# Norm sums one chunk later in layer 0, and an end with a fixed order and its norm weights on GpSimd

## The chip, the cores and the metric

One NeuronCore of a Trainium2 chip runs the whole program in one launch. The metric is the device time of one execution in microseconds. Engine names here are PE (TensorE, matmuls), DVE (VectorE), ACT (ScalarE), POOL (GpSimd) and SP (SyncE, which only issues DMAs). Each engine works through its own queue in the order in which the program was built, and waits at an instruction until the semaphores named there have been raised.

## The reference

512 tokens of width 1024 go through two layers and a last norm. All is float32.

```python
# layer 0: h += conformer_conv(rmsnorm(h)); h += swiglu_ffn(rmsnorm(h))
# shared K/V from rmsnorm(h); layer 1: h += attention; h += swiglu_ffn(rmsnorm(h))
def rmsnorm(x, g):
    return x * lax.rsqrt(jnp.mean(x * x, axis=-1, keepdims=True) + EPS) * g
def swiglu_ffn(x, w_up, w_down):
    gate, up = jnp.split(x @ w_up, 2, axis=-1)
    return (jax.nn.silu(gate) * up) @ w_down      # inner width 2816
return rmsnorm(h, norm_final)
```

## The kernel before

The residual stream lies transposed in `hT` (channels on the partitions, tokens along the free axis) until the last layer's FFN, where blocks of it are flipped to tokens on the partitions. Weights come in chunks of 128 x 1024 floats (0.5 MB) in the order of one list, `PLAN`. SP loads a chunk nine places ahead into one of six `raw` buffers. Three places ahead each chunk is split in two float32r parts: ACT casts the high part (`whi`, L294), DVE subtracts to get the low part (`wlo`, L297), into four buffers each. A product is then three matmuls (`mm3`, L380 to L382: high x high, high x low, low x high). Chunks of the first part (`NATIVE`, which ends with the first pair of FFN up-chunks) are not split and use one plain float32 product (L378).

RMSNorm is not applied to the FFN's input. The matmuls work on the unscaled stream, and the scale goes into the evictions. `Rms` makes it in steps: `add` squares each of the eight channel tiles on ACT (L487) and adds it to a running sum (L491, on DVE for this norm). `step1` sums over the partitions with matmuls against a column of ones (L503), makes mean plus epsilon on DVE (L505), takes the power -1/2 on POOL (L507) and, for 256 tokens, puts the scales on two diagonal matrices on ACT (L515). `spread` multiplies these with a matrix of ones (L529), so that each partition has every token's scale, and `step2` copies that to SBUF (L523).

Layer 0's first FFN runs on 256 tokens at a time. For the first half of the tokens (`ffn_part(0, 0, ...)`, not `twin`) `ffn_up` goes over pairs of column blocks; a pair has four chunks (two halves of the inner dimension times gate and up), 24 matmuls each when split. The first pair's eviction is held in `pending`, and done inside the second pair: `step1` stands behind the first pair, and the evictions, with the spread, behind the second chunk of the second pair (line 697). At the same time DVE, ACT and POOL make the depthwise convolution of the other half of the tokens (L1010 on DVE, L1002 on ACT, L1003 on POOL, squares and sums L1039 to L1045), and POOL issues DMAs that add weight blocks in memory (L289), which a counter spreads over the chunks.

The second half of the tokens (`twin`) and layer 1 use other paths; the diff leaves them as they are.

At the very end layer 1's last pair is multiplied out with tokens on the partitions. For each of four blocks of 128 tokens and each of two halves of 512 channels (`g`) PE makes six matmuls into a bank (L1600). DVE scales it and adds the residual (L1602). ACT squares it and sums along the row (L1604). DVE makes the mean from both halves (L1606, L1608), POOL the power (L1610). DVE multiplies by the norm's weights (L1611), and the scale goes on last, one half on ACT (L1617), the other on DVE (L1615), each followed by its output DMA (L1618) from ACT's queue or SP's. No order is written down there: a scheduler put the instructions of the four blocks into each engine's queue by its own estimates.

Of the kernel before, what the change touches and what calls it, by code (L numbers as in the profile page):

```python
# [11 lines left out]
F32 = mybir.dt.float32  # L12
F32R = mybir.dt.float32r
AF = mybir.ActivationFunctionType
ALU = mybir.AluOpType
# [3 lines left out]
P = 128  # L19
D = 1024  # L20
# [8 lines left out]
NBLK = S // P  # L29
BAND = 2 * P  # L30
NBUCKET = 32
EPS = 1e-6
# [177 lines left out]
def hybrid_trunk(ctx: ExitStack, tc: tile.TileContext, xT, W, prm_in, wdw_in, sinks, relb, onehot, fin, lead, out):  # L210
    nc = tc.nc
    cpool = ctx.enter_context(tc.tile_pool(name="const", bufs=1))
    quads = ctx.enter_context(tc.tile_pool(name="quads", bufs=11))
    wpool = ctx.enter_context(tc.tile_pool(name="wts", bufs=4))
    tmp = ctx.enter_context(tc.tile_pool(name="tmp", bufs=5))
    small = ctx.enter_context(tc.tile_pool(name="small", bufs=4))
# [15 lines left out]
    def temp():  # L232
        return tmp.tile([P, 512], F32, tag="tmp", name=uid("tmp"))
# [128 lines left out]
    def get(*key):  # L362
        advance()
        pace()
        due[0] += rate[0]
        tick(int(due[0]))
        due[0] -= int(due[0])
        i = stream["use"]
        assert PLAN[i] == key, (PLAN[i], key)
        stream["use"] += 1  # L370
        hi, lo = splits.pop(i)
        n = {"kv": 4, "up": 4, "q": 4}.get(key[0], 2)
        sh = dict(a=n)
        return tuple(w and w.rearrange("p (a b) -> p a b", **sh) for w in (hi, lo))
# [95 lines left out]
    mhalf = cpool.tile([P, 4], F32, tag="mhalf", name="mhalf")  # L470
# [414 lines left out]
    def rows_of(g, t):  # L885
        return hT[:, g * 4:(g + 1) * 4, t * P:(t + 1) * P]
# [386 lines left out]
    class Rows0:  # L1273

        rms = None
# [46 lines left out]
    nxt = Next(("kv", "mix1"))  # L1322
# [5 lines left out]
    for pair, a in part2_products():  # L1328
        if pair not in open_pairs:
            c = z0.tile([P, 2, 2, 2, 256], F32, tag="z0", name=uid("up"), bufs=5)  # L1330
# [5 lines left out]
        c = open_pairs[pair].gates()  # L1336
# [15 lines left out]
    if True:  # L1352
# [6 lines left out]
        x, rms = nxt.x, nxt.rms  # L1359
# [8 lines left out]
        for half in range(2):  # L1368
            whi, wlo = get("kv", 0, half)
# [7 lines left out]
        for half in range(2):  # L1377
            whi, wlo = get("kv", 1, half)
            for k in range(4):
                xh, xl = xkv[half * 4 + k]  # L1380
# [4 lines left out]
            if half == 0:  # L1385
                rs_bc = rms.step2()
                rs = rms.rs
# [133 lines left out]
        for part in range(2):  # L1521
            for g in range(2):
# [3 lines left out]
                if part == 0:  # L1526
# [19 lines left out]
                for m in range(4):  # L1546
                    i = g * 4 + m
                    nc.vector.tensor_add(h[i], banks[m], h[i])
                    nxt.on_h(i)
            if part == 0:  # L1550
# [4 lines left out]
                nxt = Rows("ffn1", pool7)  # L1555
# [12 lines left out]
    for kind, pair in STEPS1:  # L1568
# [6 lines left out]
        if by_seven(1, pair):  # L1575
            c = seven_pair("up", pair, nxt, new_gates(pool7), flip if pair == SEVENS[0] else None)
# [11 lines left out]
        nc.sync.dma_start(gain, fin.to_broadcast([P, D]))  # L1588

    whole = [get("down", 1, LAST, g) for g in range(2)]  # L1590
    for b in range(NBLK):
        tok, rs = slice(b * P, (b + 1) * P), nxt.rms.rs[:, b:b + 1]
        room = quads.tile([P, 4, 512], F32, tag="quad", name=uid("room"))
        ss = small.tile([P, 4], F32, tag="ss", name=uid("ss"))
        for g, (whi, wlo) in enumerate(whole):
            acc = bank()
            for k in range(2):
                xh, xl = (hid[:, e, k, tok] for e in range(2))
                for n, (x, w) in enumerate(((xh, whi), (xh, wlo), (xl, whi))):
                    nc.tensor.matmul(acc, x, w[:, k, :], start=k == 0 and n == 0, stop=k == 1 and n == 2)  # L1600
            v, o = room[:, g], room[:, 2 + g]
            nc.vector.scalar_tensor_tensor(v.rearrange("p (i c) -> p i c", i=4), acc.rearrange("p (i c) -> p i c", i=4), rs,  # L1602
                                           rows_of(g, b), op0=ALU.mult, op1=ALU.add)
            nc.scalar.activation(temp(), v, AF.Square, accum_out=ss[:, g:g + 1])  # L1604
            if g == 0:
                nc.vector.tensor_scalar(ss[:, 2:3], ss[:, 0:1], 1.0 / D, EPS, op0=ALU.mult, op1=ALU.add)  # L1606
            else:
                nc.vector.scalar_tensor_tensor(ss[:, 3:4], ss[:, 1:2], 1.0 / D, ss[:, 2:3], op0=ALU.mult, op1=ALU.add)  # L1608
                last = small.tile([P, 1], F32, tag="rs1", name=uid("rs1"))
                nc.gpsimd.tensor_tensor(last, ss[:, 3:4], mhalf[:, 0:1], op=ALU.pow)  # L1610
            nc.vector.tensor_mul(o, v, gain[:, g * 512:(g + 1) * 512])  # L1611
        for g in range(2):
            o = room[:, 2 + g]
            if g:
                nc.vector.tensor_scalar(o, o, last[:, 0:1], None, op0=ALU.mult)  # L1615
            else:
                nc.scalar.mul(o, o, last[:, 0:1])  # L1617
            (nc.sync if g else nc.scalar).dma_start(out[tok, g * 512:(g + 1) * 512], o)  # L1618
    seven.close()


# [25 lines left out]
```

## Time and profile before

| | |
|---|---|
| median of 3 runs | 1046.09 us (1045.9 to 1046.29) |
| profiled execution | 1048.36 us |
| its span, first to last instruction | 1046.6 us |
| granted TensorE clock, mean | 0.997 |
| PE / DVE / ACT / POOL busy | 1032.7 / 779.1 / 612.7 / 466.6 us |
| instructions | 17683 |

In a timeline row the first number is the start in us from the span's start, the second the length from the first to the last of the merged instructions; then engine, line, operation, what is written and read, shape, and the count. Square brackets give the idle time of the engine ahead of the row and what ended it. In the rows for one tile three numbers stand for the shortest, the median and the longest duration in ns. In the list of waits the columns are the total in us, the number of times and the longest one.

### The profile page before, as it was taken

To read this page: it belongs to the slowest core of one execution; us is meant where nothing else is said; L and a number is where in the kernel's file an instruction comes from. 1 tells how busy PE (TensorE), PEld (TensorE's weight loads), DVE (VectorE), ACT (ScalarE), POOL (GpSimd) and SP (SyncE) were. 2 spreads that over 40 slices of the span, in tenths; PEclk is the share of its full clock that TensorE was granted. 3 is DMA by queue.
4 is the path that set the end of the run, shared out by engine and by line. 5 is a ranking of instruction groups with operands and counts; after the bars stand their busy time and mean duration, and the time that the engine had idled before them with its cause. 6 is when DMAs were issued, how large, how long until landed. Compare 5 with 4: busy or idle time off the path is not lost.

```text
span 1046.6 us, 17683 instructions
## 1 busy us (share of the span) xinstructions
PE 1032.7 (99%) x6574; PEld 932.7 (89%) x6574; DVE 779.1 (74%) x1206; ACT 612.7 (59%) x1060; POOL 466.6 (45%) x563
## 2 busy tenths in 40 slices
PE   9999998999999999999999999999999999999996
PEld 8888887999988999998888877788989999898995
DVE  3999989978889786773536556678686877868677
ACT  3887896946776565552334555466655555554653
POOL 3999998940444332222214255405442334334131
PEclk9999999999999999999999999999999999999998
DMA  9999846989899988898968776845879888867742
GB/s 351 335 332 195 203 130 173 282 245 272 243 256 253 302 221 283 255 296 251 284 222 240 208 192 183 211 167 150 251 234 312 284 264 266 244 232 222 226 142 80
DMA packets 67282, 248.33 MB, mean 237 GB/s; under 512 B 7579, under 2 KB 13884, under 8 KB 66364
## 3 DMA queue, kind: packets, MB, share of 16 engines
q1 hardware_dynamic: 53804, 199.96, 54.7%
q0 software_dynamic: 12672, 46.14, 24.6%
q8 instruction: 51, 0.84, 0.3%
q10 hardware_dynamic: 720, 1.10, 0.3%
q14 instruction: 35, 0.29, 0.1%
HBM read 241.93 MB, written 97.52 MB: 324 GB/s over the span
## 4 chain that ended last, share of the span: by engine, by line
PE 91%; DVE 4%; ACT 2%; issue 1%; DMA 1%; POOL 1%; SPq 0%; DVEq 0%; ACTq 0%
PE bank L380 20%; PE bank L382 20%; PE bank L381 20%; PE bank L903 9%; PE bank L961 8%; PE bank L412 4%; PE bank L413 2%; PE bank L1442 1%; PE bank L1484 1%; PE bank L1471 1%; DVE bank L1010 1%; ACT pr L1002 1%; PE bank L1059 1%; DVE wlo L297 1%; DMA both<-in_lead_dram 1%
## 5 line engine op out<-in xcount | busy, mean ns | idle before, releaser
L297 DVE TENSOR_TENSOR wlo<-raw,whi 128x1024 fp32r<-128x1024 f32 x246 | 327.1, 1337 | 137.7 <-ACT whi L294 126.9
L294 ACT CAST whi<-raw 128x1024 fp32r<-128x1024 f32 x246 | 257.2, 1049 | 280.9 <-PE bank L381 194.9
L380 PE MATMUL bank<-quad,whi 128*128 128x256 f32 (+1 forms) x976 | 307.2, 317 | 0.0
L381 PE MATMUL bank<-quad,whi 128*128 128x256 f32 (+1 forms) x976 | 306.6, 315 | 0.0
L382 PE MATMUL bank<-quad,wlo 128*128 128x256 f32 (+1 forms) x976 | 305.7, 315 | 0.0
L380 PEld LDWEIGHTS bank<-quad,whi 128*128 128x128 f32 x976 | 185.5, 191 | 12.8 <-issue 1.6
L381 PEld LDWEIGHTS bank<-quad,whi 128*128 128x128 f32 x976 | 186.0, 191 | 11.8 <-issue 0.5
L382 PEld LDWEIGHTS bank<-quad,wlo 128*128 128x128 f32 x976 | 185.6, 191 | 11.8 <-issue 0.4
L854 POOL TENSOR_TENSOR up<-up 128x512 f32<-128x512 f32 x34 | 62.9, 1851 | 283.6 <-ACT up L851 283.6
L1003 POOL TENSOR_TENSOR pr<-pr,pr 128x256 f32<-128x256 f32 x208 | 157.5, 837 | 4.5 <-ACT pr L1002 4.2
L380 PE MATMUL bank<-rows,whi 128*128 128x256 f32 x488 | 138.0, 283 | 0.0
L381 PE MATMUL bank<-rows,whi 128*128 128x256 f32 x488 | 137.8, 282 | 0.0
L382 PE MATMUL bank<-rows,wlo 128*128 128x256 f32 x488 | 137.8, 282 | 0.0
L1010 DVE SCALAR_TENSOR_TENSOR bank<-apad,wdw,bank 128x256 f32<-128x256 f32 x248 | 112.4, 484 | 3.4
L1002 ACT ACTIVATE pr<-apad,wdw 128x256 f32<-128x256 f32 x208 | 98.5, 502 | 15.1 <-POOL pr L1003 13.2
L961 PE MATMUL bank<-quad,w 128*128 128x256 f32 x448 | 98.7, 380 | 0.0
L961 PEld LDWEIGHTS bank<-quad,w 128*128 128x128 f32 x448 | 84.9, 190 | 11.8 <-DVE bank L1010 0.2
L380 PEld LDWEIGHTS bank<-rows,whi 128*128 128x128 f32 x488 | 93.1, 191 | 0.3
L381 PEld LDWEIGHTS bank<-rows,whi 128*128 128x128 f32 x488 | 93.1, 191 | 0.3
L382 PEld LDWEIGHTS bank<-rows,wlo 128*128 128x128 f32 x488 | 93.0, 191 | 0.0
L491 POOL TENSOR_TENSOR tmp<-tmp,tmp 128x256 f32<-128x256 f32 (+1 forms) x28 | 26.8, 956 | 101.9 <-ACT tmp L487 96.7
L412 PE MATMUL bank<-quad,whi 128*128 128x512 f32 x168 | 59.7, 398 | 0.0
(229 smaller groups left out, 1632.9 us busy)
## 6 DMA issues: line engine op xcount, KB each, us to landing
raw<-in_W_dram SPq DMA_DIRECT2D x170, 512.0 KB, 5.7
raw<-sum SPq DMA_DIRECT2D x88, 512.0 KB, 5.5
sum<-in_W_dram SPq DMA_DIRECT2D x52, 512.0 KB, 6.3
sum<-in_W_dram POOLq DMA_DIRECT2D x44, 512.0 KB, 9.5
sum<-sum POOLq DMA_DIRECT2D x44, 512.0 KB, 8.8
sum<-in_W_dram SPq DMA_DIRECT2D x4, 3584.0 KB, 29.7
w<-in_W_dram SPq DMA_DIRECT2D x14, 512.0 KB, 9.7
sum<-in_W_dram SPq DMA_DIRECT2D x4, 1024.0 KB, 29.6
```

The lines of the kernel that those rows point to most:

```text
L294: on_act = nc.scalar.copy(hi, src).ins
L297: latest[:] = [on_act, lo_engine[0].tensor_sub(lo, src, f32(hi)).ins]
L380: nc.tensor.matmul(out, w[0], x[0], start=start, stop=False, **kw)
L381: nc.tensor.matmul(out, w[0], x[1], start=False, stop=False, **kw)
L382: nc.tensor.matmul(out, w[1], x[0], start=False, stop=stop, **kw)
L412: nc.tensor.matmul(first[2], first[0], first[1], start=start, stop=False)
L854: pool_op(nc.gpsimd.tensor_mul(gate, gate, c[:, m, :, 1, :]))
L903: nc.tensor.matmul(out, x, w[:, ws], start=first and e == 0 and i == 0, stop=e == 1 and i == 2, skip_group_check=True)
L961: mm = nc.tensor.matmul(self.pb[:, w * W2:(w + 1) * W2], w1_of(ct, w, k), x[k] if x else xg[k][:, tok], start=k == 0, stop=k == KT - 1)
L1002: on_act = nc.scalar.mul(pr, a[:, j:j + W2], tap(j))
L1003: on_pool = pool_op(nc.gpsimd.tensor_add(pr, acc, pr))
L1010: on_dve = nc.vector.scalar_tensor_tensor(yt if i == nd - 1 else c, src, tap(i), c if i else self.shift, op0=ALU.mult, op1=ALU.add)
```

## The change

In `ffn_up`, when a first pair is pending, `step1` now stands behind the first chunk of the second pair instead of behind the first pair, and the pending evictions (with the spread) behind its third chunk instead of its second. The path for `twin` keeps its places.

The end is rewritten. `piece` makes the matmuls of one block's half or part of it, and each engine's instructions there are chained (`tc.issue_after`) in the order of the program text: PE, DVE, ACT and POOL each get a fixed order. The last block's second half is split into two pieces of 256 channels, with a bank, an eviction and a sum of squares each, so the mean has three steps there. The norm weights of the first three blocks, both halves, are multiplied by POOL; those of the last block stay on DVE. A block's scaling and output stand two blocks later in the text. Outputs leave from SP's queue, but for the last block's first half, which leaves from ACT's.

```diff
-                    if half == 0 and which == 1:
-                        if w == 512 or twin:
-                            rms.step1()
+                    if twin and half == 0 and which == 1 or pending and half + which == 0:
+                        rms.step1()
+                    if half == 1 and which == 0:
                         for p in pending:
                             evac(*p)
                         pending = []
-            if w == 256 and pair == lo and not twin:
-                rms.step1()
+            if pair == lo and not twin:
                 pending.append((pair, full))
...
+    def piece(b, g, i0, i1):
+        room, ss, _ = blocks[b]
+        cols, rs = slice(i0 * P, i1 * P), nxt.rms.rs[:, b:b + 1]
+        acc = bank()[:, 0:(i1 - i0) * P]
...                                   # the six matmuls, after order["t"]
+        v, s = room[:, g, cols], ss[:, g + i0 // 2:g + i0 // 2 + 1]
+        then("v", lambda: nc.vector.scalar_tensor_tensor(...))        # was L1602
+        then("s", lambda: nc.scalar.activation(temp()[:, cols], v, AF.Square, accum_out=s))   # was L1604
...                                   # mean (DVE), power (POOL) as before, by then()
+    def weigh(b, g, eng, op):
+        room = blocks[b][0]
+        then(eng, lambda: op(room[:, 2 + g], room[:, g], gain[:, g * 512:(g + 1) * 512]))
+    def scale(b, g):
+        o, last = blocks[b][0][:, 2 + g], blocks[b][2]
+        if g:
+            then("v", lambda: nc.vector.tensor_scalar(o, o, last[:, 0:1], None, op0=ALU.mult))
+        else:
+            then("s", lambda: nc.scalar.mul(o, o, last[:, 0:1]))
+        (nc.sync if g or b < ends else nc.scalar).dma_start(out[...], o)
+    for b in range(NBLK):
+        blocks.append([...])
+        if b > 1:
+            scale(b - 2, 0)
+        piece(b, 0, 0, 4)
+        if b:
+            mean(b - 1, 1)
+        if b < ends:
+            weigh(b, 0, "p", nc.gpsimd.tensor_mul)
+        if b:
+            power(b - 1, 1)
+        if b == ends:
+            break
+        piece(b, 1, 0, 4)
+        mean(b, 0)
+        weigh(b, 1, "p", nc.gpsimd.tensor_mul)
+        if b > 1:
+            scale(b - 2, 1)
+    scale(ends - 2, 1)
+    piece(ends, 1, 0, 2)
+    piece(ends, 1, 2, 4)
+    weigh(ends, 0, "v", nc.vector.tensor_mul)
+    for n in range(3):
+        mean(ends, n)
+    power(ends, 2)
+    scale(ends - 1, 0)
+    weigh(ends, 1, "v", nc.vector.tensor_mul)
+    scale(ends - 1, 1)
+    scale(ends, 0)
+    scale(ends, 1)
```

In the built order PE's L503 stands 24 matmuls later than before and L529 24 matmuls later as well; DVE's queue is the same up to L505 and beyond it to the first eviction. In ACT's queue one L294 and two L1002 stand ahead of L515 that stood behind it, and in POOL's queue two L289 stand ahead of L507 behind the pair of L1014 where one did.

More of the change, by code (lines that the diff above doesn't have):

```diff
@@ L1590, in hybrid_trunk @@
     whole = [get("down", 1, LAST, g) for g in range(2)]
-    for b in range(NBLK):
[L1592 to L1618, printed above, removed]
@@ new lines, in hybrid_trunk, with then @@
+    order = {}
+    def then(eng, op):
+        with tc.issue_after(order[eng]) if eng in order else nullcontext():
+            order[eng] = op().ins
+    blocks, ends = [], NBLK - 1
+    def piece(b, g, i0, i1):
+        room, ss, _ = blocks[b]
+        cols, rs = slice(i0 * P, i1 * P), nxt.rms.rs[:, b:b + 1]
+        whi, wlo = whole[g]
+        acc = bank()[:, 0:(i1 - i0) * P]
+        with tc.issue_after(order["t"]) if "t" in order else nullcontext():
+            for k in range(2):
+                xh, xl = (hid[:, e, k, b * P:(b + 1) * P] for e in range(2))
+                for n, (x, w) in enumerate(((xh, whi), (xh, wlo), (xl, whi))):
+                    mm = nc.tensor.matmul(acc, x, w[:, k, cols], start=k == 0 and n == 0, stop=k == 1 and n == 2)
+        order["t"] = mm.ins
+        v, s = room[:, g, cols], ss[:, g + i0 // 2:g + i0 // 2 + 1]
+        then("v", lambda: nc.vector.scalar_tensor_tensor(
+            v.rearrange("p (i c) -> p i c", c=P), acc.rearrange("p (i c) -> p i c", c=P), rs,
+            rows_of(g, b)[:, i0:i1], op0=ALU.mult, op1=ALU.add))
+        then("s", lambda: nc.scalar.activation(temp()[:, cols], v, AF.Square, accum_out=s))
@@ new lines, in mean, with power @@
+    def mean(b, n):
+        ss = blocks[b][1]
+        if n == 0:
+            then("v", lambda: nc.vector.tensor_scalar(ss[:, 4:5], ss[:, 0:1], 1.0 / D, EPS, op0=ALU.mult, op1=ALU.add))
+            return
+        then("v", lambda: nc.vector.scalar_tensor_tensor(ss[:, 4 + n:5 + n], ss[:, n:n + 1], 1.0 / D, ss[:, 3 + n:4 + n],
+                                                         op0=ALU.mult, op1=ALU.add))
+    def power(b, n):
+        blocks[b][2] = last = small.tile([P, 1], F32, tag="rs1", name=uid("rs1"))
+        then("p", lambda: nc.gpsimd.tensor_tensor(last, blocks[b][1][:, 4 + n:5 + n], mhalf[:, 0:1], op=ALU.pow))
@@ new lines, in weigh @@
+    def weigh(b, g, eng, op):
[7 more added lines that the diff above has]
+            then("s", lambda: nc.scalar.mul(o, o, last[:, 0:1]))
+        (nc.sync if g or b < ends else nc.scalar).dma_start(out[b * P:(b + 1) * P, g * 512:(g + 1) * 512], o)
```

2 lines of the change are left out of this document (added).

## The prediction

> **What bounds the kernel now.** I read the page's busy times first, then the list of what TensorE (PE) waited for, then the timelines of each engine around the two places that the diff touches.
>
> ```profile
> PE 1032.7 (99%) x6574; PEld 932.7 (89%) x6574; DVE 779.1 (74%) x1206; ACT 612.7 (59%) x1060; POOL 466.6 (45%) x563
> ...
> PE bank L529 <- ACT tmp L515: 2.1, 1, 2.1
> ...
> PE bank L503 <- DVE tmp L491: 1.0, 1, 1.0
> ```
>
> PE is busy for all but 13.9 us of the 1046.6 us span. Its list of waits holds, besides start-up, only these two, both in layer 0's first FFN half: the matmuls that sum the squares (L503) and the one that spreads the scale (L529). Whatever shortens the kernel takes away one of these or the tail behind the last matmul. The profiled execution took 1048.36 us, 1.8 around its span; the three times have a median of 1046.09. I work out differences inside the span and take them off the median. 0.2% of it, 2.1 us, is about what a measurement of this kernel can tell from no change.
>
> **First place: sums and spread one chunk later.** PE's timeline:
>
> ```profile
> 163.77 9.23 PE L378 MATMUL bank<-plain,raw 128*128 128x256 f32 x42
> 174.05 0.61 PE L503 MATMUL bank<-ones_c,tmp 128*128 128x1 f32 x4 [1.05 <-DVE tmp L491]
> ...
> 174.96 0.28 PE L380 MATMUL bank<-quad,whi 128*128 128x256 f32 x1
> ...
> 180.23 0.28 PE L382 MATMUL bank<-quad,wlo 128*128 128x256 f32 x1
> 182.63 0.70 PE L529 MATMUL bank<-tmp,ones_m 128*128 128x256 f32 x2 [2.13 <-ACT tmp L515]
> 182.98 0.47 PE L380 MATMUL bank<-quad,whi 128*128 128x256 f32 x1
> ```
>
> PE stands 1.05 us before L503 and 2.12 before L529, with 48 matmuls (two chunks) between. From 174.96 to 180.23 there are 44 steps, so one matmul costs 0.12 us and a chunk of 24 costs 2.88. The built order shows one chunk moved ahead of L503, and still two chunks between L503 and L529. Now the other engines:
>
> ```profile
> 171.49 2.50 DVE L491 TENSOR_TENSOR tmp<-tmp,tmp 128x256 f32<-128x256 f32 x1
> 173.92 5.12 DVE L297 TENSOR_TENSOR wlo<-raw,whi 128x1024 fp32r<-128x1024 f32 x3
> 178.96 2.05 DVE L1010 SCALAR_TENSOR_TENSOR bank<-apad,wdw,bank 128x256 f32<-128x256 f32 x4
> 180.92 0.15 DVE L505 TENSOR_SCALAR ms<-bank 128x2 f32<-128x2 f32 x1
> 183.55 1.23 DVE L297 TENSOR_TENSOR wlo<-raw,whi 128x1024 fp32r<-128x1024 f32 x1 [2.48 <-ACT whi L294]
> ...
> 181.89 0.69 ACT L515 ACTIVATE tmp<-ident,rs 128x128 f32<-128x128 f32 x2 [7.29 <-POOL rs L507]
> 182.49 1.03 ACT L294 CAST whi<-raw 128x1024 fp32r<-128x1024 f32 x1
> ...
> 177.90 0.81 POOL L289 DMA_DIRECT2D sum<-in_W_dram  x1
> 178.47 1.17 POOL L1045 TENSOR_TENSOR sq<-sq,sq 128x256 f32<-128x256 f32 x1
> 181.15 0.71 POOL L507 TENSOR_TENSOR rs<-ms,mhalf 128x2 f32<-128x2 f32 x1 [1.51 <-DVE ms L505]
> ```
>
> What holds L529 is not L503: VectorE (DVE) works without a gap from 171.49 to 181.07, and L505, which reads L503's sums, is simply ninth in its queue. In the changed order L505 has the same place behind the same three L297 and four L1010. So L505 stays at 180.92, L507 at 181.15, L515 at 181.89 and L529 can start at 182.63, as before, though L503 ends later. PE meanwhile goes straight from L378 into the next chunk: 2.88 us to about 175.7, where the last L491 (done 173.99) no longer holds L503. L503 and 48 more matmuls took 174.05 to 180.51, that is 6.46 us, and now end at 182.2. About 0.4 us of the wait before L529 is left. When L529 runs PE has done 72 matmuls instead of 48: gain 24 x 0.12 = **2.9 us**. It cannot exceed the two waits, 3.2, and would shrink by whatever L515 comes later.
>
> What else moves: on ScalarE (ACT) the cast L294 and two taps L1002 go ahead of L515. They need 1.03 + 2 x 0.5 us and have ACT's 7.29 us gap; the cast must wait until the first chunk has left its buffer, about 175.8, and is done by 177.8, 4 us before the scales arrive. On GpSimd (POOL) one more DMA issue (L289, 0.81 us) stands before L507, whose queue had 1.51 us to spare. It costs nothing; without that cover it would cost 0.8. DVE loses its 2.48 us gap at 183.55, since the cast it waited for is already made, so the splits keep pace with PE's lead. First evictions come one chunk later in PE's order, and their banks too. PE has no wait between 183 and the end in the list, so I let the 2.9 us reach the tail whole.
>
> **Second place: the end.**
>
> ```profile
> 1027.78 0.61 PE L1600 MATMUL bank<-whi,hid 128*128 128x512 f32 x2
> 1037.07 0.39 PE L1600 MATMUL bank<-whi,hid 128*128 128x512 f32 x1
> ...
> L1602 DVE SCALAR_TENSOR_TENSOR room<-bank,rs,h x8: 741/746/752, 1026.4 to 1038.5; 128x512 f32<-128x512 f32 x8
> L1611 DVE TENSOR_TENSOR room<-room,gain x8: 676/684/692, 1027.7 to 1039.9; 128x512 f32<-128x512 f32 x8
> L1615 DVE TENSOR_SCALAR room<-room,rs x4: 478/484/490, 1035.0 to 1041.6; 128x512 f32<-128x512 f32 x4
> ...
> 1039.88 0.68 DVE L1611 TENSOR_TENSOR room<-room,gain 128x512 f32<-128x512 f32 x1
> ...
> 1036.28 0.56 POOL L1610 TENSOR_TENSOR rs<-ss,mhalf 128x1 f32<-128x1 f32 x1 [1.81 <-DVE ss L1608]
> 1039.98 1.56 POOL L1610 TENSOR_TENSOR rs<-ss,mhalf 128x1 f32<-128x1 f32 x2 [3.14 <-DVE ss L1606]
> ...
> 1041.02 1.33 ACT L1617 ACTIVATE room<-room,rs 128x512 f32<-128x512 f32 x2 [1.03 <-POOL rs L1610]
> 1041.77 0.95 ACTq L1618 DMA_DIRECT2D out_dram<-room  x2
> ...
> L1010 DVE SCALAR_TENSOR_TENSOR bank<-apad,wdw,bank 128x256 f32<-128x256 f32 x248 | 112.4, 484 | 3.4
> ```
>
> The last matmul ends at 1037.46, but the last eviction starts only at 1038.5, behind queued multiplications, and the last output is issued by 1042.72. The change takes six of the eight L1611 (0.6 us a step, 3.7 us in all) from DVE and gives them to POOL, in front of the powers L1610. The price there lies between two POOL rows of the same size:
>
> ```profile
> L910 POOL TENSOR_TENSOR h<-h,tmp x10: 1287/1296/1842, 781.1 to 1020.4; 128x512 f32<-128x512 f32 x10
> L854 POOL TENSOR_TENSOR up<-up x34: 1288/1944/2312, 353.5 to 1017.2; 128x512 f32<-128x512 f32 x34
> ...
> 1019.13 2.55 POOL L910 TENSOR_TENSOR h<-h,tmp 128x512 f32<-128x512 f32 x2
> 1019.98 0.75 DVE L912 SCALAR_TENSOR_TENSOR h<-bank,rs,h 128x512 f32<-128x512 f32 x1 [1.96 <-PE bank L903]
> ...
> 7.30 0.62 DVE L923 TENSOR_SCALAR quad<-both,prm 128x256 f32<-128x256 f32 x2 [2.45 <-DMA both<-in_lead_dram]
> 8.54 1.09 DVE L923 TENSOR_SCALAR quad<-both,prm 128x256 f32<-128x256 f32 x2 [0.62 <-DMA both<-in_lead_dram]
> ...
> 7.85 3.23 POOL L491 TENSOR_TENSOR tmp<-tmp,tmp 128x256 f32<-128x256 f32 x4 [2.07 <-ACT tmp L487]
> ```
>
> I take 1.30 us: L910 runs in the same stretch, beside the same kind of eviction (L912, 0.75 us beside it, as long as L1602 without). But a scaling (TENSOR_SCALAR) suffers beside POOL: two L923 took 1.09 us instead of 0.62.
>
> In before's clock: 42 matmuls from 1027.78 to 1037.07 are 0.227 us apart, so block 0's second half is in its bank at 1029.30, its eviction ends at 1030.1, and from 1030.17 POOL works without a gap: five multiplications and two powers up to 1030.17 + 5 x 1.30 + 2 x 0.57 = 1037.8. Block 3's first half is evicted by 1036.9. Then DVE's queue has block 1's scaling (its power is ready at 1036.5), which meets POOL's fifth multiplication and ends about 0.3 us behind it, 1038.1. Queued behind it are the two new half evictions (256 wide: 484 ns as L1010, which also reads a bank, and some 0.4 from one start to the next; their banks are full at 1036.9 and 1037.5, since twelve matmuls at 0.12 take as long as six at 0.227): done 1039.0. One multiplication to 1039.5, three steps on single columns to 1040.1. The power takes 1.0 us, as the first of the two at 1039.98 did beside the multiplication of 1039.88: 1041.15. ACT's scaling, 0.72, and an issue of 0.34 us end at 1042.3 instead of 1042.72: **0.4 us** gained. Unblocked scaling and a 0.56 us power would give 1.4; a POOL multiplication of w us changes it by 5 (w - 1.30).
>
> The Trainium skill ("SBUF — State Buffer", Who interferes with whom) says that such a scaling and a POOL instruction exclude each other for the whole instruction, whoever comes first. By that the scaling's full 0.48 us would follow, and the gain at the end be 0.2 us. The two L923, stretched by 0.47 together, don't decide between a block of the whole and of a part.
>
> Sum: 2.9 + 0.4 = 3.3, so **1042.8 us**.
>
> **Rivals.**
> *The spread moves with the sums.* If what counts is the 8.6 us from L503 to L529, L529 comes later by as much as L503 does, and only the first wait goes: 1046.09 - 1.05 - 0.4 = 1044.6. For it: the two are parts of one chain. Against it: DVE's queue, full to 181.07. Chance 0.06.
>
> *PE's lead is given back in layer 0 or later*, when PE meets weights or banks that DVE or ACT release no sooner: 1046.09 - 0.4 = 1045.7. Against it: DVE's and ACT's gaps here close too. Chance 0.05.
>
> *POOL's multiplications are dear.* If they take L854's mean of 1.85 us (62.9 us for 34), the end loses 2.3 instead of gaining 0.4: 1045.5, no change that shows; chance 0.05. From w = 1.97 the end's loss eats the first place's 2.9; at L854's longest, 2.31, the end loses 4.6: 1046.09 - 2.9 + 4.6 = 1047.8. For it: L854's median is 1.94, and each multiplication stands ahead of the powers and, by these, of DVE's and ACT's queues. Against it: L910. Chance 0.04. The Trainium skill ("GPSIMD Engine Reference", Engine selection) advises against POOL for elementwise work with two inputs, about twice as slow; 1296 against 684 ns agrees.
>
> That PE keeps the old order is excluded by the built order.
>
> **How the numbers follow.** The forecast has 0.80; its own range, from 3.2 + 1.4 gained to 2.4 gained and 0.4 lost, is 1041.5 to 1044.1. To cover what the unlisted may take from its ends I go to 1041.3, and over the first rival to 1045.0, which leaves out some 2 in 10. Faster by over 0.2% (under 1044.0): 0.80. Within: 0.06 + 0.05 + 0.05 = 0.16. Slower: 0.04.
>
> **What would show it.** In the changed profile PE's waits have no row for L503 and one of under 1 us for L529; L505 still stands at 180.9. POOL's multiplications show 1.3 us, and block 1's scaling more than 0.48. Wrong if L529 stands later than 183.0, if PE's list has a new wait behind it, or if the last matmul ends less than 2.5 us earlier.

## The result, and the profile after

The changed kernel took 1043.61 us (median of 12 runs, 1042.96 to 1045.43), the kernel before 1046.05 (12 runs, 1045.59 to 1046.54): a ratio of 0.9979, interval 0.9970 to 0.9988. The profiled execution took 1043.27, with a span of 1041.5. Measured again later, the same two kernels stood at 1044.95 and 1045.87, ratio 0.9990 (0.9981 to 0.9999). So the gain is 2.44 us once and 0.92 the other time. The main finding of this study is a contest between two engines that an execution of the changed kernel can win or lose, for 1.25 us; why the two measurements drew it so differently stays open.

In the profile after, the two waits that the prediction started from are gone. The busy times first, then PE's waits, which hold start-up alone:

```profile
PE 1031.5 (99%) x6580; PEld 932.6 (90%) x6580; DVE 776.5 (75%) x1202; ACT 613.0 (59%) x1062; POOL 473.2 (45%) x569
```

```profile
PE bank L465 <- POOL ones_m L462: 1.1, 1, 1.1
PE bank L948 <- DVE quad L922: 0.7, 2, 0.4
```

The timelines of the engines around the first place, in the kernel after. Lines of the file from 706 to 1587 are one lower than in before (L1009 for L1010, L1002 for L1003); each row is start, duration, engine, line, with the idle time ahead of it in brackets:

```profile
172.17 0.47 PE L380 MATMUL bank<-quad,whi 128*128 128x256 f32 x1
...
175.23 0.50 PE L503 MATMUL bank<-ones_c,tmp 128*128 128x1 f32 x4
...
181.43 0.59 PE L529 MATMUL bank<-tmp,ones_m 128*128 128x256 f32 x2
...
168.83 0.95 DVE L491 TENSOR_TENSOR tmp<-tmp,tmp 128x256 f32<-128x256 f32 x1
169.70 5.18 DVE L297 TENSOR_TENSOR wlo<-raw,whi 128x1024 fp32r<-128x1024 f32 x3
174.80 2.05 DVE L1009 SCALAR_TENSOR_TENSOR bank<-apad,wdw,bank 128x256 f32<-128x256 f32 x4
176.76 0.15 DVE L505 TENSOR_SCALAR ms<-bank 128x2 f32<-128x2 f32 x1
...
178.61 0.71 POOL L507 TENSOR_TENSOR rs<-ms,mhalf 128x2 f32<-128x2 f32 x1
...
179.35 0.69 ACT L515 ACTIVATE tmp<-ident,rs 128x128 f32<-128x128 f32 x2 [2.19 <-POOL rs L507]
```

PE goes straight from the first pair into the next chunk, then L503, then L529, with nothing missing. But L505 stands at 176.76, not at 180.92 where the prediction wanted it, with the same three L297 and four L1009 ahead of it. The last L491 ran 0.95 us here at 168.83; in before it ran 2.50 us at 171.49. VectorE was less late, and this in a stretch of its queue that the change does not touch.

The end, in the kernel after:

```profile
1033.05 0.28 PE L1607 MATMUL bank<-whi,hid 128*128 128x256 f32 x1
...
1029.21 2.55 POOL L1629 TENSOR_TENSOR room<-room,gain 128x512 f32<-128x512 f32 x2
1031.31 0.74 DVE L1634 TENSOR_SCALAR room<-room,rs 128x512 f32<-128x512 f32 x1
...
1032.43 1.28 POOL L1629 TENSOR_TENSOR room<-room,gain 128x512 f32<-128x512 f32 x1
1032.62 1.10 DVE L1620 SCALAR_TENSOR_TENSOR ss<-ss 128x1 f32<-128x1 f32 x1
1033.65 0.47 DVE L1634 TENSOR_SCALAR room<-room,rs 128x512 f32<-128x512 f32 x1
1034.05 0.86 DVE L1610 SCALAR_TENSOR_TENSOR room<-bank,rs,h 128x256 f32<-128x256 f32 x2
...
1036.03 0.69 DVE L1629 TENSOR_TENSOR room<-room,gain 128x512 f32<-128x512 f32 x1
1036.19 0.96 POOL L1625 TENSOR_TENSOR rs<-ss,mhalf 128x1 f32<-128x1 f32 x1 [1.66 <-DVE ss L1620]
1037.18 0.72 ACT L1636 ACTIVATE room<-room,rs 128x512 f32<-128x512 f32 x1 [1.05 <-POOL rs L1625]
1037.94 0.34 ACTq L1637 DMA_DIRECT2D out_dram<-room  x1
```

GpSimd's multiplication takes 1.28 us and the last power 0.96, as forecast. The step L1620 adds two single columns. It takes 0.15 us when GpSimd is quiet, and 1.10 here: it ends when the multiplication ends. The scaling L1634 and the last evictions L1610 queue behind it, so that even the first of these starts 1.0 us after the last matmul began, though its bank was full before that.

The spans of the two profiles differ by 5.1 us, twice what the medians do, because the profiled execution of before took 2.3 us more than the median of its kernel (1048.36 us against 1046.05). So I compare by landmarks. The program falls into parts: start-up, to the first spread (the first L529); from there to the spread of the second token half (L529 at some 280 us), which holds the first place; from there to the first matmul of the end (L1600, L1607 in after); from that to the end of the last DMA issue; and what is left of the span. Fourteen profiles, read from their timelines (us; the last column is the profiled execution's time):

| kernel | start-up | first place | middle | end | behind it | time |
|---|---|---|---|---|---|---|
| before | 18.61 | 264.10 | 740.96 | 19.05 | 3.8 | 1048.36 |
| before, again (r1) | 18.29 | 261.63 | 740.94 | 19.05 | 3.8 | 1045.54 |
| after | 18.14 | 260.38 | 740.95 | 18.81 | 3.2 | 1043.27 |
| after, again (r3) | 18.85 | 261.67 | 740.96 | 18.78 | 3.2 | 1045.27 |
| first place only (e1) | 18.79 | 261.64 | 740.95 | 19.06 | 3.8 | 1046.04 |
| first place only, again (r2) | 18.52 | 261.67 | 740.95 | 19.05 | 3.8 | 1045.79 |
| end only (e2) | 18.64 | 261.66 | 740.95 | 18.82 | 3.2 | 1045.06 |
| sums later (e3) | 18.15 | 260.39 | 740.95 | 19.05 | 3.8 | 1044.14 |
| spread later (e4) | 18.09 | 260.70 | 740.96 | 19.05 | 3.8 | 1044.42 |
| after, no split (e6) | 18.02 | 261.67 | 740.95 | 18.48 | 3.3 | 1044.23 |
| sums later, fused end (e7) | 17.83 | 260.40 | 740.94 | 17.57 | 3.4 | 1041.92 |
| after, weights on DVE, two copies (e8) | 18.64 | 260.38 | 740.96 | 18.42 | 3.2 | 1043.38 |
| after, free order at the end (e9) | 18.66 | 260.39 | 740.95 | 19.48 | 3.2 | 1044.46 |
| first place only, two copies (e10) | 18.41 | 260.39 | 740.94 | 19.06 | 3.8 | 1044.42 |

Three things are to be seen. The middle is the same to 0.02 us in all of them: whatever PE gains in the first place arrives at the end whole, so both places can be changed in one run and read apart. The changed end gives 0.24 us to the last issue and some 0.6 behind it, in all three of its profiles (after, r3, e2). And the first place takes 260.4 us when PE waits nowhere in it (260.7 in e4, with no wait listed), and 261.65 in two of the three profiles of before's order (r1, e2) *and in four of the six of the changed order*. 264.10 was seen once; times like that execution's (1048.18 and 1048.48 us) came twice more among the runs of before, without a profile. Start-up differs by up to 1.0 us from one execution to the next, whatever the kernel, and was not looked into: single times, without the landmarks, say little here.

### The profile page after: what moved, and what is told of

Same layout as the page of the kernel before. It is cut to its first block, busy times and chain, and to the rows that moved or that the text cites. A ratio compares the mean times of both kernels' runs of the same rounds, so it can differ in the third digit from the quotient of the medians.

```text
span 1041.5 us, 17709 instructions
## 1 busy us (share of the span) xinstructions
PE 1031.5 (99%) x6580; PEld 932.6 (90%) x6580; DVE 776.5 (75%) x1202; ACT 613.0 (59%) x1062; POOL 473.2 (45%) x569
## 4 chain that ended last, share of the span: by engine, by line
PE 98%; DMA 0%; DVE 0%; issue 0%; POOLq 0%; SPq 0%; POOL 0%; ACT 0%
PE bank L380 20%; PE bank L382 20%; PE bank L381 20%; PE bank L960 10%; PE bank L902 9%; PE bank L412 4%; PE bank L378 4%; PE bank L413 2%; PE bank L1441 1%; PE bank L1483 1%; PE bank L1470 1%; PE bank L1058 1%; PE bank L1607 1%; PE bank L948 1%; DMA both<-in_lead_dram 0%; PE bank L1562 0%
## 5 line engine op out<-in xcount | busy, mean ns | idle before, releaser
L297 DVE TENSOR_TENSOR wlo<-raw,whi 128x1024 fp32r<-128x1024 f32 x246 | 329.7, 1348 | 136.8 <-ACT whi L294 136.5
L294 ACT CAST whi<-raw 128x1024 fp32r<-128x1024 f32 x246 | 257.1, 1049 | 276.6 <-PE bank L381 194.1
L382 PE MATMUL bank<-quad,wlo 128*128 128x256 f32 (+1 forms) x976 | 305.7, 315 | 0.0
L382 PEld LDWEIGHTS bank<-quad,wlo 128*128 128x128 f32 x976 | 185.6, 191 | 11.8 <-issue 0.4
L1002 POOL TENSOR_TENSOR pr<-pr,pr 128x256 f32<-128x256 f32 x208 | 155.4, 788 | 2.6 <-ACT pr L1001 2.5
L382 PE MATMUL bank<-rows,wlo 128*128 128x256 f32 x488 | 137.8, 282 | 0.0
L1009 DVE SCALAR_TENSOR_TENSOR bank<-apad,wdw,bank 128x256 f32<-128x256 f32 x248 | 112.4, 485 | 3.4
L1001 ACT ACTIVATE pr<-apad,wdw 128x256 f32<-128x256 f32 x208 | 98.3, 502 | 14.9 <-POOL pr L1002 13.1
L382 PEld LDWEIGHTS bank<-rows,wlo 128*128 128x128 f32 x488 | 93.0, 191 | 0.0
L491 POOL TENSOR_TENSOR tmp<-tmp,tmp 128x256 f32<-128x256 f32 (+1 forms) x28 | 26.8, 957 | 101.4 <-ACT tmp L487 96.2
```

Source lines behind the costliest of these rows:

```text
L294: on_act = nc.scalar.copy(hi, src).ins
L297: latest[:] = [on_act, lo_engine[0].tensor_sub(lo, src, f32(hi)).ins]
L382: nc.tensor.matmul(out, w[1], x[0], start=False, stop=stop, **kw)
L1001: on_act = nc.scalar.mul(pr, a[:, j:j + W2], tap(j))
L1002: on_pool = pool_op(nc.gpsimd.tensor_add(pr, acc, pr))
L1009: on_dve = nc.vector.scalar_tensor_tensor(yt if i == nd - 1 else c, src, tap(i), c if i else self.shift, op0=ALU.mult, op1=ALU.add)
```

## The experiments

**Each place by itself (e1, e2).** e1 has only the edit in `ffn_up`, e2 only the end.

> Only the first place changed (sums and spread one chunk later), the end as before. Theory A (PE needs one more chunk of cover, and both waits go): no row for L503 or L529 in PE's waits, 2.1 to 2.9 us gained, so 1043.2 to 1044.0 us, and the last issue still ends 5.3 us after the last matmul. Rival B (the end's fixed order made the gain): 1045.6 to 1046.5 us, no gain that shows. Rival C (the 2.1 us wait of the profiled execution of before was a stretch of VectorE's sums by chance, and the median held less): a gain of about 1 us, 1045 us.

> Only the end changed, the first place as before. Theory A: PE's waits show L503 (about 1.0 us) and L529 (about 2.1) again, the last issue ends some 0.3 us less after the last matmul than in before, 1045.7 us. Rival B: 1043.6 us. Rival C: the same time as A, but the two waits of the first place differ from before's by over 1 us in sum, since this execution draws another stretch of L537 and L491 (before: 3.25 and 2.50 us; after: 0.95 each).

Measured: e1 1045.95 us against 1045.70, ratio 1.0003 (0.9994 to 1.0011); e2 1044.86, ratio 0.9993 (0.9984 to 1.0002). So the first place alone gave nothing here, and theory A fell although both its waits are gone from e1's list. (The time is rival B's, but B wanted 1043.6 us of e2.) In their stead stands this wait, in e1's waits of PE:

```profile
PE bank L382 <- DVE wlo L297: 1.0, 1, 1.0
```

In e2, whose first place is that of before, L503 does not wait and L529 waits 1.0 us instead of 2.1 (expected by C, not by A). Of the end, theory A's 0.3 us to the last issue came out as 0.24, but the time fell by 0.84: another 0.6 lies behind the last issue, where I had looked for nothing.

**Sums or spread alone (e3, e4).**

```diff
 e3, against after:
     -if half == 1 and which == 0:      # evictions, spread
     +if half == 0 and which == 1:      # at before's place
 e4, against before: rms.step1() stays behind the first pair
     -if half == 0 and which == 1:      # evictions, spread
     +if half == 1 and which == 0:      # one chunk later
```

> In before, the sums (step1) one chunk later, the spread and evictions at their old place: 72 matmuls lie ahead of the spread as in the changed kernel less 24, so 48 and all of them ahead of it at the same time as in before. Theory A (the spread's time is set by VectorE's queue, not by the sums): L503's wait goes, L529's grows by as much to about 3.2 us, no gain: 1046.0 us. Rival D (the spread follows the sums by a chain of 8.6 us): L529 moves later by 1.8 us with L503, 1047.9 us. Rival E (moving the sums shortens VectorE's queue ahead of L505, which stood at 176.8 in the changed kernel and at 180.9 in before): L529 waits under 1 us, 1043.6 to 1044.3 us.

> In before, the sums at their old place, the spread and evictions one chunk later. Theory A: L503 still waits 1.0 us, L529 (72 matmuls after L503) no longer: 2.1 us gained, 1043.9 us. Rival D (chain from the sums): the same 2.1 us. Rival E: L505 stays at about 180.9, because the sums were not moved; the wait at L529 still goes, by its cover. Rival C: under 1 us gained, if the wait is mostly shorter than in the profiled execution of before.

Measured: e3 1044.70 us, ratio 0.9989 (0.9980 to 0.9998), and e4 1044.67, ratio 0.9990 (0.9981 to 0.9999). Neither shows a wait of PE behind start-up, and both gain 1.0 us. For e3 theory A expected no gain, on the premise that only 48 matmuls lie ahead of the spread. The trace shows otherwise. In e3's timeline of PE:

```profile
172.19 0.47 PE L380 MATMUL bank<-quad,whi 128*128 128x256 f32 x1
...
175.24 0.50 PE L503 MATMUL bank<-ones_c,tmp 128*128 128x1 f32 x4
175.61 0.36 PE L380 MATMUL bank<-quad,whi 128*128 128x256 f32 x1
...
180.24 0.59 PE L529 MATMUL bank<-tmp,ones_m 128*128 128x256 f32 x2
```

From the sums to the spread there are 4.63 us (175.61 to 180.24) where the changed kernel has 5.83 for its 48 matmuls: 1.2 us less, ten matmuls, so 38. With the chunk ahead of the sums that makes 62 in front of the spread, against 48 in before and 72 in the changed kernel. So e3 did not move the sums alone: in the built order its spread also stands 14 matmuls later, 1.7 us, where e2, with the order of before, waits 1.0. Rival E, an earlier L505, does not explain the gain either: L505 stands at 176.68 in e3 and at 176.57 in e4, where the sums were not moved. The spread's cover of PE work suffices for both runs; what the place of the sums does by itself was not measured. And the time of the spread was never fixed at 182.6: that was a property of one execution.

**The same kernels again (r1, r2, r3).** No edit: before, first place only, and the whole change.

> The kernel before, once more, for a second profile. From the first spread (L529, at 18.6 us) to the spread of the second token half (L529, at 282.7) the first profile of before took 264.1 us, the kernel with only the end changed, whose code is the same there, 261.7. Theory F (the two waits of the first place grow and shrink with how long VectorE's operations are held up beside GpSimd's trains of L1003, so the profiled execution of before was an unlucky one): 261 to 262.5 us here, the waits at L503 and L529 together 0.5 to 2 us and not 3.2, time 1045.2 to 1046.3. Theory A as predicted (the waits belong to the order): 264 us and 3.2 us of waits again.

> Only the first place changed, once more. Theory F: the wait of 1.0 us at L382 (201.2 us), behind a split L297 of 4.34 us, is another draw of the same hold-up, so it is gone or elsewhere here: 260.4 to 261.7 us between the two spreads, 1043.9 to 1046.0 us in all. Rival G (the changed order always runs into that L297): the wait stands at the same place with about 1.0 us and the time is 1046 us again.

> The whole change, once more. Theory F: no wait at L503 or L529, 260.4 us between the two spreads, or up to 1.3 more if an L297 is held up; 0.24 us less than before from the end's first matmul to the last issue and 0.65 less behind it; 1043.1 to 1044.2 us. Rival G: a wait at L382 at about 201 us, 1045 us.

Measured: before 1045.87 us, first place only 1045.92 (ratio 1.0001, 0.9992 to 1.0010), the whole change 1044.95 (0.9990, 0.9981 to 0.9999). The second profile of before:

```profile
168.86 0.95 DVE L491 TENSOR_TENSOR tmp<-tmp,tmp 128x256 f32<-128x256 f32 x1
...
172.51 0.50 PE L503 MATMUL bank<-ones_c,tmp 128*128 128x1 f32 x4
179.84 0.70 PE L529 MATMUL bank<-tmp,ones_m 128*128 128x256 f32 x2 [0.97 <-ACT tmp L515]
...
176.78 0.15 DVE L505 TENSOR_SCALAR ms<-bank 128x2 f32<-128x2 f32 x1
...
178.10 0.96 POOL L507 TENSOR_TENSOR rs<-ms,mhalf 128x2 f32<-128x2 f32 x1
```

Here L503 does not wait, L505 stands at 176.78 (176.5 to 177.3 in all later profiles, as start-up shifts it), and what is left is 0.97 us ahead of L529. In the first profile of before this row of VectorE stands ahead of the L491 of 2.50 us:

```profile
161.36 3.25 DVE L537 SCALAR_TENSOR_TENSOR quad<-h,prm,quad 128x256 fp32r<-128x256 f32 x1
```

In the second profile no L537 of this stretch takes more than 0.95. So the before that the change has to beat is 1.25 us over the floor of 260.4, not 3.7. And in r2 and r3 the changed order gives just that back: the wait of 1.0 us at L382 was there again, with 261.67 us, as rival G had it. Theory F had it gone or elsewhere in r2; in r3 its bound of up to 1.3 us more covers the stretch, but 1044.95 us lies over its 1044.2. In the second profile of the whole change:

```profile
201.27 0.39 PE L382 MATMUL bank<-quad,wlo 128*128 128x256 f32 x1 [1.03 <-DVE wlo L297]
...
196.86 4.35 DVE L297 TENSOR_TENSOR wlo<-raw,whi 128x1024 fp32r<-128x1024 f32 x1
...
195.69 4.44 POOL L1002 TENSOR_TENSOR pr<-pr,pr 128x256 f32<-128x256 f32 x6
```

and in the first profile of it, at the same instructions:

```profile
196.13 1.61 DVE L297 TENSOR_TENSOR wlo<-raw,whi 128x1024 fp32r<-128x1024 f32 x1
...
194.95 6.49 POOL L1002 TENSOR_TENSOR pr<-pr,pr 128x256 f32<-128x256 f32 x6
```

An L297 alone takes 1.22 us. GpSimd adds six pairs of tap products in a row. In the bad case these run at 0.70 us each, 4.44 in all, and L297, which came 1.17 us after their start, ends 1.08 behind their end: it stood aside for all that was left of the train. In the good case L297 comes just as late (1.18), but gets in behind the second addition: the third then takes 1.81 us, and GpSimd's six 6.49. PE needs that low part at 200.2, hence the wait of 1.03.

What differs is a pause. The third addition starts when ACT's product (L1001) is there, 0.65 us behind that instruction's start in each of these profiles, or when the second is done. From the second addition's start to the third's it was 0.70 us (r3), 0.78 (e6), 0.79 (e1) and 0.80 (r2) where L297 was held for 4.34 to 4.37 us, and 0.87 (e9), 0.88 (after) and 0.93 (e4) where it took 1.60 or 1.61. Up to here G, a wait that comes with the order, is not refuted: most profiles of the order have it.

**Making the pause (e8, e10).** To test this, ACT was given two copies of four columns ahead of the four products, in the whole change (e8, with all weights of the end on VectorE besides) and in the first place alone (e10):

```diff
 on_act = nc.scalar.copy(hi, src).ins
+nudge[0] += 1
+if nudge[0] == 11:
+    for _ in range(2):
+        with tc.issue_after(on_act):
+            on_act = nc.scalar.copy(warm, warm).ins
 e8 also: -weigh(b, g, "p", nc.gpsimd.tensor_mul)  +weigh(b, g, "v", nc.vector.tensor_mul)
```

The rivals J and K in the first text are about the end, and are set out with e7 below: whether GpSimd's multiplications hold VectorE up there (J) or relieve it (K).

> The whole change, with two edits. First: two copies of four columns on ScalarE (0.19 us each) behind the eleventh cast L294, ahead of the four products that feed GpSimd's train of six additions at about 195.7 us. Theory F in its sharper form (an L297 on VectorE waits until GpSimd's train breaks; in the good profile of the whole change the third addition found its product some 0.04 us late, in the bad ones 0.13 to 0.23 early): the products come 0.2 to 0.4 us later, the train breaks, that L297 takes 1.2 to 1.8 us instead of 4.35 and PE's wait at L382 is gone: 260.4 to 260.7 us between the two spreads and not 261.67. Rival G: the wait is there with 1.0 us. Second: at the end all weights on VectorE, with the fixed order and the split kept. Theory J: the last issue ends about 18.1 us from the end's first matmul (the whole change 18.8); rival K: 19.0 or more. With theory F and J 1042.9 to 1043.6 us, with G and K 1045.2.

> The first place as in the change, the end as in before, and the two copies on ScalarE behind the eleventh cast: the first place's gain by itself. Without the copies this kernel twice showed no gain (1045.95 and 1045.92 us against 1045.70 and 1045.87), with a wait of 1.0 us at L382 in both profiles and a pause of only 0.10 to 0.11 us in GpSimd's train ahead of its third addition. Theory F: the copies open that pause to some 0.2 us or more, the L297 at 196 to 197 us takes 1.6 us instead of 4.35, L382 does not wait, 260.4 to 260.7 us lie between the two spreads instead of 261.65, and the time is 1.0 us below that of before (1044.7 to 1045.0), with the end's 19.05 us unchanged. Rival G (the wait comes from the order, not from that pause): 261.65 us and no gain. Rival L (before's own wait at L529 is often absent, so that there is nothing to gain in most executions): the wait at L382 is gone, and the time still within 0.3 us of before's.

Measured: e10 1044.44 us against 1046.11, ratio 0.9983 (0.9974 to 0.9992); e8 1042.80, ratio 0.9971 (0.9959 to 0.9982). In e10's timelines (lines five higher than in after):

```profile
196.17 0.41 ACT L299 COPY warm<-warm 128x4 f32<-128x4 f32 x2
...
195.22 1.69 POOL L1007 TENSOR_TENSOR pr<-pr,pr 128x256 f32<-128x256 f32 x2
197.13 2.18 POOL L1007 TENSOR_TENSOR pr<-pr,pr 128x256 f32<-128x256 f32 x2 [0.22 <-ACT pr L1006]
...
196.40 1.60 DVE L302 TENSOR_TENSOR wlo<-raw,whi 128x1024 fp32r<-128x1024 f32 x1
```

The products come 0.33 us later, the train breaks, L297 (L302 here) takes 1.60 and PE does not wait: 260.39 us. All 11 runs of e10 lie at 1043.96 to 1045.16; the 22 runs of the same kernel without the copies (e1, r2, on other chips) lay at 1045.27 to 1046.58. *Work added to ACT saves some 1.5 us* between these medians, 1.25 by the first place's column. So the wait hangs on the pause and not on the order alone: G falls, and theory F stands in its sharper form. Rival L falls too, since e10 is clear of before by its interval. That all of e10's 1.67 us comes from there is not shown: the profiles of before are too few to say how often it draws more than 1.0 us of waits (its 15 runs beside e10 reached from 1045.32 to 1048.48).

**The end (e6, e7, e9, and e8's weights).**

```diff
 e6: -piece(ends, 1, 0, 2); piece(ends, 1, 2, 4)
     +piece(ends, 1, 0, 4)                       # and two steps of mean()
 e9: -with tc.issue_after(order[eng]) ...        # in then() and piece()
 e7: first place as e3; no split, no weights on GpSimd;
     -weigh(b, 1, ...); tensor_scalar(o, o, last, None, mult)
     +scalar_tensor_tensor(o, v, last, gain, mult, mult)
     weigh(b, 0) on VectorE; scale(b - 1, *) right behind piece(b, 1)
```

> The whole change without the split of the last half block: one eviction of 512 columns (0.74 us) and one square (0.62 + 0.19) in the place of two of 256 (0.86 and 0.40 + 0.19 behind the second). The last eviction starts with the last matmul instead of overlapping it: the last sums come about 0.3 us later by theory A, and with them the last issue, which then ends about 0.1 us behind before's (19.1 us from the end's first matmul) instead of 0.24 ahead. Rival H (the split brings nothing, since the last evictions stand behind the scaling that waits for GpSimd): no difference from the whole change, 18.8 us.

> The whole change, with the end's fixed order taken out: the scheduler orders the instructions of the blocks, weights stay on GpSimd and the split stays. The built order puts block 0's second weights third in GpSimd's queue, behind those of block 1. If the order matters by what it feeds GpSimd (its five last multiplications then run from about 7.6 to 15.2 us from the end's first matmul, and block 1's scaling behind them), the last issue ends at 19.3 to 20.0 us and the time is 0.5 to 1.2 us over that of the whole change, 1045.4 to 1046.1. If the order is worth nothing: 18.8 us, 1044.9. The first place is that of the whole change: L382 waits 1.0 us in most executions.

> Another version of both places. First place: sums one chunk later, spread at its old place. Theory F: 260.4 us between the two spreads and no wait at L382, as in the one earlier profile of that order. End: no weights on GpSimd and no split; one VectorE instruction (value x scale x weight, about 0.7 us) takes the place of the weight and the scaling of each second half, the first halves' weights are multiplied on VectorE (0.6 us a step), and the scalings of a block stand one half block earlier. Theory J (what cost the changed end its gain is that VectorE's steps on two inputs in SBUF are held up by GpSimd's multiplications: 1.10 us instead of 0.15 for the sums of block 2, 0.71 instead of 0.48 for a scaling): without them the last eviction starts within 0.3 us of its bank instead of 0.8 to 1.1 late, and the last issue ends 17.3 to 17.6 us from the end's first matmul (before 19.05, the whole change 18.8): 1042.0 to 1043.0 us. Rival K (GpSimd's multiplications are a relief that VectorE needs): VectorE falls behind its banks and the last issue ends at 18.8 us or later: 1043.5 us or more.

Measured by the end's column, from 18.8 us of the whole change. *No split* (e6; 1044.81 us): 18.48, so the split costs 0.3, against theory A and rival H. The last eviction starts no later without it, since it waits behind the held L1620 either way, and one single-column step fewer lies in the chain. Behind the last issue 0.1 of it is lost again (3.3 against 3.2). *Weights on VectorE* (e8): 18.42, so GpSimd's six multiplications cost 0.38; theory J in kind, with half its size. There the step beside them is not held, in e8's timeline:

```profile
1033.70 0.15 DVE L1625 SCALAR_TENSOR_TENSOR ss<-ss 128x1 f32<-128x1 f32 x1
1033.77 0.47 DVE L1639 TENSOR_SCALAR room<-room,rs 128x512 f32<-128x512 f32 x1
```

*Free order* (e9): 19.48, so the fixed order is worth 0.67, the one part of the end that pays. Its 1044.46 us are less than the 1045.4 to 1046.1 expected, for which L382 was to wait: in the profile its L297 was not held. Without the fixed order block 0's scaling meets GpSimd's fifth multiplication and the sums of block 2 its sixth, in e9's timeline:

```profile
1031.97 1.42 DVE L1633 TENSOR_SCALAR room<-room,rs 128x512 f32<-128x512 f32 x1
...
1034.36 0.70 DVE L1619 SCALAR_TENSOR_TENSOR ss<-ss 128x1 f32<-128x1 f32 x1
```

Each of these figures is what one part is worth with the others in place, so they do not add up to the end's 0.24.

*Fused* (e7): 17.57, as theory J expected, and 1042.15 us against 1046.10, ratio 0.9966 (0.9952 to 0.9979; 5 runs): faster than before. It was not measured beside the changed kernel, whose end takes 1.24 us more. Of these the weights and the split, by e8 and e6, would make 0.7; what the fused instruction and the earlier scalings do was not taken apart. Its last half block, with its bank full at 1032.96:

```profile
1033.20 0.74 DVE L1610 SCALAR_TENSOR_TENSOR room<-bank,rs,h 128x512 f32<-128x512 f32 x1
...
1034.79 0.16 DVE L1620 SCALAR_TENSOR_TENSOR ss<-ss 128x1 f32<-128x1 f32 x1
...
1035.03 0.55 POOL L1625 TENSOR_TENSOR rs<-ss,mhalf 128x1 f32<-128x1 f32 x1 [1.34 <-DVE ss L1620]
```

The eviction starts 0.24 us late (in e6, also without a split, 0.78), and the power takes 0.55 with no multiplication of VectorE beside it.

**Behind the last issue.** No run was made for this alone. The outputs' DMA lines in the profiles of before and of after:

```profile
DMA to landing us min/median/max: 2.0/2.3/3.3
```

```profile
DMA to landing us min/median/max: 2.0/2.0/2.6
```

Before issues its last four outputs from 1041.54 to 1042.38, within 0.84 us; after issues them from 1036.16 to 1037.94, within 1.78. The longest landing that the view has is 0.7 us shorter, close to the 0.6. That the spacing is the cause is an inference: in all fourteen profiles the kernels with before's end have 3.8 and those with the blocks' outputs spread out 3.2 to 3.4. But the spread of the last four does not order the latter: e9 has 3.2 with 1.44 us, e7 has 3.4 with 1.70.

## Why the prediction was right, and which of its steps were not

The forecast was 1042.8 us in a range of 1041.3 to 1045.0. Both measurements, 1043.61 and 1044.95, lie in it, the second by 0.05 us. The likeliest case, under 1044.0, is that of the first alone. The sum was 3.3 us, 2.9 from the first place and 0.4 from the end. The profiles show 0 to 1.25 for the first place and 0.85 for the end, 0.24 to the last issue and 0.6 behind it. By medians the first place can be worth more (2.44 less e2's 0.84 leaves 1.6; e10 has 1.67), and what makes up that rest is open.

- *Both waits go.* Right in all profiles of the changed order, and L529 keeps no rest of 0.4.
- *"L505 stays at 180.92."* Wrong. It is at 176.76 in after and at 176.78 in before's second profile. The queue ahead of it was read rightly; its time was that of an execution in which L537 had been held for 3.25 us and L491 for 2.50. With L505 early, GpSimd's queue holds L507 (178.61 in after), and the DMA issue moved ahead of it costs nothing there either, as PE comes to L529 later still (181.43).
- *Gain 24 x 0.12 = 2.9.* This is the term that was mis-sized. 3.2 us of waits stood in a profile that was 2.27 us over its kernel's median, and I took differences inside that span off the median without asking where the 2.27 lay. They lay in these very waits: against the second profile of before no more than 1.25 us was there to win.
- *The gain reaches the tail whole.* The middle of 740.95 us shows that nothing behind 280 us takes it. But in four of the six profiles of that very order PE gives 1.0 us back at L382, 19 us behind L529. That is the rival "PE's lead is given back", to which I gave 0.05, in kind as it was written: PE meets a low part that VectorE releases late. My ground against it, that VectorE's gap at 183.55 closes, counted VectorE's work and not who holds it up. The prediction named a new wait of PE behind L529 as a sign of being wrong, and these four profiles show it.
- *The end, 0.4.* Measured 0.24. Multiplications 1.28 to 1.30 us (1.30 taken) and power 0.96 (1.0 taken) were right. The last multiplication ended 0.1 us later than in my sum, counted from the end's first matmul (14.24 against 14.13). The rest is the block. That a scaling which meets a multiplication ends 0.3 us behind it was right: block 0's does so in after (L1634 from 1031.31, 0.74 us long, ends 0.28 behind the multiplication) and in e9 (0.29). But block 1's scaling did not meet one. It queued behind block 2's L1620, which my sum did not hold up at all and which was shut out to the multiplication's end, and it ended 0.41 behind it. The Trainium skill ("SBUF — State Buffer", Who interferes with whom) has such a scaling and a GpSimd instruction shut each other out for the whole instruction, by which I had put the gain at 0.2. The trace comes near that value, but by another way, the shut-out of L1620: where a scaling did meet a multiplication, not its full 0.48 us followed but 0.28. What is left alone is L1610, which has one of its two inputs in a bank: it takes 0.75 us beside the multiplications as without.
- *What I left out:* the 0.6 us behind the last issue. I ended the sum at the issue, though the outputs' landing is part of the time, and the change alters how closely they follow each other.

So the time came out near the forecast by luck: by the profiles the first place gave less than half of its 2.9, and the end twice its 0.4. The range held for a reason it did not name: which of two ways an execution goes.

What stays open: why ten of the twelve first runs of the changed kernel lay at 1042.96 to 1044.11, as if L297 had seldom been held there, while of the second eleven ten lay above 1044.3. The first measurement has one profile of each kernel only.

## What to carry to other kernels

Ahead of costing a wait, set the profiled execution beside the median: where it stands out by as much as the gain hoped for, the wait itself may be the excess, and a second profile of the same kernel is the cheapest experiment there is. A lead that PE wins is worth what the next late operand leaves of it, so look past the wait removed for the next instruction that two engines contend for; here a pause of 0.2 us in GpSimd's train decided over 1 us of PE. Ahead of moving elementwise work to GpSimd, list what runs on VectorE beside it with both inputs in SBUF, single columns too, and scalings: in the last microseconds an end that left GpSimd only the powers did better. And count the matmuls that the built order has ahead of an instruction before an experiment is said to have moved one thing alone.

## What the hardware showed that I had not expected

A VectorE instruction with two SBUF inputs is shut out not by one GpSimd instruction but by a whole run of them: 3.1 us of waiting in front of an L297 of 1.22 us, while the rest of the second of six additions and the last four went by, 0.70 us from start to start. It got in where GpSimd's starts were 0.87 us or more apart and did not at 0.70 to 0.80; where the line lies exactly is open, as the L537 of 3.25 us in before got in at 0.80.

Size does not protect: an addition of one column went from 0.15 to 1.10 us. Nor does a single tensor input in all cases: a scaling of 0.48 us took 0.74 and 1.42 beside multiplications. And a stretch whose order is the same can so take 260.4 or 261.65 us (the changed order) and 261.65 or 264.1 (that of before) in executions at the same granted clock (0.997 or 0.998 in all fourteen profiles), while 740.95 us behind it repeat to 0.02.
